# Linear attention on one core: shared copies and spare TensorE products in the last octet, and the fourth octet stored in five pieces

## The chip, the core and the metric

The kernel runs on one core of a Trainium2 chip. The metric is the device time in microseconds (us) of one execution. The kernel before takes 126.67 us, the median of 3 runs (126.56 to 126.73). A profile shows the span from the first to the last instruction of one execution, which is some 1.8 us shorter than that execution's time.

## The reference

```python
batch, heads, seq, dim = 8, 12, 512, 64                 # Q, K, V: float32
Q_feat = np.maximum(0, Q)
K_feat = np.maximum(0, K)
KV    = np.einsum('bhkd,bhkv->bhdv', K_feat, V)
K_sum = np.sum(K_feat, axis=2)
numerator   = np.einsum('bhqd,bhdv->bhqv', Q_feat, KV)
denominator = np.einsum('bhqd,bhd->bhq', Q_feat, K_sum)
return numerator / (denominator[:, :, :, None] + 1e-10)
```

There are 96 heads. The kernel handles them in twelve groups of eight, called octets, numbered 0 to 11 in the code; "the fourth octet" is `o == 3`, and the last is `o == NO - 1 == 11`.

## The kernel before

Each octet goes through the same steps: K and V are masked and multiplied (`mm_kv`), the sums are copied out of PSUM (`evac_kv`), Q is transposed and goes through the ReLU (`qt`), numerators (`out_t`) and denominators (`denom`) are computed, the numerators are transposed back (`back`), divided (`norm`) and stored (`store`). The order on each engine is the order of the program. All stores are issued by SyncE. Cuts are marked with `...`.

```python
    def evac_kv(o, gs):                       # four copies, all on ScalarE
        for s in range(2):
            for c in range(2):
                nc.scalar.copy(kvd[o % NK][64 * c:64 * c + 64, ...], ps_kv[64 * s:64 * s + 64, gs, ...])

    def qt(o):                                # Q transposed, ReLU on the way out of PSUM
        for i in range(2):
            ...                               # eight transposes into ps_qt
            if o == NO - 1 and i == 1:
                nc.vector.tensor_scalar(..., op0=Alu.max)
            else:
                nc.scalar.activation(qt_sb[o % NZ][:, us], ps, Act.Relu)

    def out_t(o):                             # numerators, two halves of four products each
        for j in range(2):
            ps = pou.tile([P, 4, U, 16], fp32, name="ps_ot", tag="ps_out")
            ...
            copy = nc.vector.tensor_copy if o == NO - 1 and j == 1 else nc.scalar.copy
            copy(ot[o][:, :, 4 * j:4 * j + 4], ps.rearrange("p h u c -> p u h c"))

    def store(o, o_sb):
        if o + DELAY < NO:
            nc.sync.dma_start(out=scratch, in_=k_sb[2 * (o + DELAY)][0:1, 0, :])
        Ov = Or[o].rearrange("p (r d) -> p r d", d=D)
        if o == NO - 1:                       # the last octet: two halves
            for j in range(2):
                rs = slice(RQ // 2 * j, RQ // 2 * (j + 1))
                nc.sync.dma_start(out=Ov[:, rs], in_=o_sb[:, rs])
            return
        nc.sync.dma_start(out=Ov, in_=o_sb)   # 1 MB: 128 partitions of 8 KB

    ...                                       # the end of the program, o = 10
    evac_kv(o + 1, slice(0, 1))
    prep(g + 1)
    prep_v(g + 1, nc.vector)
    backs(o)                                  # both halves: transposes back, norm, store
    mm_kv(g + 1)
    evac_kv(o + 1, slice(1, 2))
    qt(o + 1)
    out_t(o + 1)
    denom(o + 1)
    backs(o + 1)
```

The small store into `scratch` makes SyncE's queue wait for a later load; it only paces the stores.

## Time and profile before

| | before |
|---|---|
| time, median of 3 | 126.67 us |
| span of the profile | 124.92 us |
| TensorE, VectorE, ScalarE busy | 69%, 65%, 63% of the span |
| DMA engines busy | 90% or more in 37 of 40 slices |
| last landing of a store | 124.00 us |

The lines below are from the page of the profile before: the granted clock of TensorE and the busy share of the sixteen DMA engines, each over 40 slices of the span (a digit is a tenth), and a row of the store's issues (count, KB each, median us from issue to landing).

```profile
PEclk9999999999999999999859999657999999999687
DMA  3999999999999999999999999999999999999984
out_dram<-o_sb SPq DMA_DIRECT2D x11, 1024.0 KB, 9.1
```

No compute engine is near full, the DMA engines are full nearly throughout, and a store lands long after its issue: it stands in a queue. The clock falls in three places: near 62 us, near 79 us, and in the tail from 116 us on. The tail of the chain, the clock in it and the last three stores are shown inside the prediction below.

### The profile page before, as it was taken

Reading aid. Unit: us, or ns where it says so; the run is one execution under the profiler, and the core shown is the slowest. Engines: PE = TensorE matmul, PEld = TensorE weight load, DVE = VectorE, ACT = ScalarE, POOL = GpSimd, SP = SyncE. Lnnn points to the kernel's source line nnn. Section 1 sums busy time; section 2 is a strip of 40 time slices with the busy share of each in tenths; the row PEclk is TensorE's granted clock in tenths of the full one; section 3 lists DMA queues with packets and bytes.
Section 4 is the critical chain, followed back from the end, with each engine's and each line's share of the span. In section 5 each row is a group of like instructions: output and inputs, shape, how many; then the busy total and the mean of one; then the engine's idle time right before and its main releaser. Section 6 shows DMA issues by size and latency. Waiting matters only on the chain.

```text
span 124.9 us, 2637 instructions
## 1 busy us (share of the span) xinstructions
PE 86.0 (69%) x1056; PEld 78.7 (63%) x1056; DVE 81.6 (65%) x175; ACT 78.9 (63%) x115; POOL 31.3 (25%) x62
## 2 busy tenths in 40 slices
PE   0032297998989899894598596199867757795640
PEld 0041285997878789793597494199756566694630
DVE  2256644749798897979348759532946936994670
ACT  0163369969898998989339589164929928647000
POOL 6902424315253331142133124034022000000000
PEclk9999999999999999999859999657999999999687
DMA  3999999999999999999999999999999999999984
GB/s 102 380 310 214 215 207 210 217 205 214 207 212 211 208 217 326 255 216 297 286 213 284 304 211 252 332 212 234 339 226 217 323 259 216 314 425 420 428 352 197
DMA packets 10748, 32.68 MB, mean 262 GB/s; under 512 B 1392, under 2 KB 1392, under 8 KB 9328
## 3 DMA queue, kind: packets, MB, share of 16 engines
q0 software_dynamic: 8064, 17.83, 74.6%
q1 hardware_dynamic: 2384, 13.63, 27.2%
q10 hardware_dynamic: 288, 1.05, 2.1%
q8 instruction: 8, 0.13, 0.4%
q14 instruction: 4, 0.03, 0.1%
HBM read 37.75 MB, written 12.58 MB: 403 GB/s over the span
## 4 chain that ended last, share of the span: by engine, by line
DMA 34%; PE 28%; DVE 26%; ACT 6%; issue 2%; SPq 0%; DVEq 0%; ACTq 0%; POOLq 0%
DMA v_sb<-in_V_dram 14%; DMA q_sb<-in_Q_dram 13%; DVE o_sb L221 12%; PE ps_kv L148 11%; PE ps_bk L215 8%; DMA kv_first<-in_K_dram 7%; PE ps_qt L171 5%; DVE kf L134 4%; ACT qt L176 4%; PE ps_ot L187 3%; ACT kvd L157 2%; DVE vo L136 2%; DVE vo L143 2%; DVE den L205 1%; DVE rec L209 1%
## 5 line engine op out<-in xcount | busy, mean ns | idle before, releaser
L148 PE MATMUL ps_kv<-vo,kf 128*128 128x132 bf16 x384 | 31.0, 246 | 17.9 <-ACT vo L141 8.2
L148 PEld LDWEIGHTS <-kf 128*128 128x128 bf16 x384 | 28.5, 110 | 19.2 <-DVE vo L136 10.9
L221 DVE TENSOR_TENSOR o_sb<-ps_bk,rec 128x1024 f32<-128x1024 f32 x24 | 28.4, 1220 | 16.7 <-PE ps_bk L215 16.7
L157 ACT CAST kvd<-ps_kv 64x260 bf16<-64x260 f32 (+1 forms) x56 | 19.2, 342 | 18.8 <-PE ps_kv L148 16.1
L176 ACT ACTIVATE qt<-ps_qt 128x1024 bf16<-128x1024 bf16 x23 | 22.4, 1026 | 6.7 <-PE ps_qt L171 6.6
L215 PE MATMUL ps_bk<-ident,ot_sb 128*128 128x128 f32 x192 | 24.5, 284 | 1.1 <-DVE ot_sb L190 1.1
L190 ACT COPY ot_sb<-ps_ot 128x1024 f32<-128x1024 f32 x23 | 23.0, 1013 | 2.9 <-PE ps_ot L187 2.0
L134 DVE TENSOR_SCALAR kf<-k_sb,mask 128x1024 bf16<-128x1024 bf16 x44 | 18.3, 457 | 7.5 <-DMA k_sb<-in_K_dram 7.5
L215 PEld LDWEIGHTS ps_bk<-ident,ot_sb 128*128 128x128 f32 x192 | 22.4, 149 | 1.1 <-ACT ot_sb L190 1.1
L92 POOL DMA_DIRECT2D k_sb<-in_K_dram x22 | 11.9, 542 | 37.9 <-DMA q_sb<-in_Q_dram 20.6
L171 PE MATMUL ps_qt<-ident,q_sb 128*128 128x128 bf16 x192 | 15.2, 243 | 7.2 <-DMA q_sb<-in_Q_dram 7.2
L171 PEld LDWEIGHTS <-q_sb 128*128 128x128 bf16 x192 | 13.7, 110 | 8.2 <-DMA q_sb<-in_Q_dram 8.0
L187 PE MATMUL ps_ot<-qt,kvd 128*128 128x256 bf16 x96 | 14.5, 283 | 5.6 <-DVE o_sb L221 4.3
L94 POOL DMA_DIRECT2D v_sb<-in_V_dram x22 | 12.4, 562 | 17.5 <-DMA k_sb<-in_K_dram 9.5
L187 PEld LDWEIGHTS <-kvd 128*128 128x128 bf16 x96 | 9.3, 100 | 8.2 <-issue 6.1
L136 DVE TENSOR_SCALAR vo<-v_sb,mask 128x1024 bf16<-128x1024 bf16 x22 | 10.7, 488 | 1.5 <-DMA v_sb<-in_V_dram 1.5
L141 ACT ACTIVATE vo<-v_sb,mask 128x1024 bf16<-128x1024 bf16 x10 | 11.5, 1154 | 0.2
L197 PEld LDWEIGHTS <-qt 128*128 128x128 bf16 x192 | 6.8, 97 | 4.4 <-ACT qt L176 3.4
L197 PE MATMUL ps_den<-kvd,qt 128*128 128x16 bf16 x192 | 7.5, 180 | 2.4 <-ACT qt L176 2.1
L98 POOL DMA_DIRECT2D q_sb<-in_Q_dram x12 | 6.5, 544 | 8.2 <-DMA v_sb<-in_V_dram 5.3
L200 DVE SCALAR_TENSOR_TENSOR own<-ps_den,mask_h 128x256 f32<-128x256 f32 x12 | 5.0, 416 | 3.3 <-PE ps_den L197 3.3
L134 DVE TENSOR_SCALAR kf<-kv_first,mask 128x1024 bf16<-128x1024 f32 x4 | 2.8, 751 | 5.1 <-DMA kv_first<-in_K_dram 5.1
(22 smaller groups left out, 26.4 us busy)
## 6 DMA issues: line engine op xcount, KB each, us to landing
out_dram<-o_sb SPq DMA_DIRECT2D x11, 1024.0 KB, 9.1
q_sb<-in_Q_dram POOLq DMA_DIRECT2D x12, 512.0 KB, 14.7
k_sb<-in_K_dram POOLq DMA_DIRECT2D x22, 256.0 KB, 14.1
v_sb<-in_V_dram POOLq DMA_DIRECT2D x22, 256.0 KB, 13.2
kv_first<-in_V_dram ACTq DMA_DIRECT2D x2, 512.0 KB, 7.3
kv_first<-in_K_dram SPq DMA_DIRECT2D x2, 512.0 KB, 6.9
out_dram<-o_sb SPq DMA_DIRECT2D x2, 512.0 KB, 2.7
scratch<-k_sb SPq DMA_DIRECT2D x7, 0.1 KB, 4.8
```

The source lines that it names most:

```text
L94: nc.gpsimd.dma_start(out=v_sb[g].rearrange("p r d -> p (r d)"), in_=Vr[g])
L134: nc.vector.tensor_scalar(kf[g][:, :, s, :], k_sb[g], scalar1=0.0, scalar2=mask[:, 0, s:s + 1], op0=Alu.max, op1=Alu.mult)
L136: nc.vector.tensor_scalar(vo[g % NB][:, :, 0, 2:D + 2], v_sb[g], scalar1=mask[:, 1, 0:1], scalar2=None, op0=Alu.mult)
L148: nc.tensor.matmul(ps_kv[:, g % 2, 0:2 * (D + 2)].rearrange("p (t d) -> p t d", t=2), kf[g][:, r, :, :].rearrange("p s d -> p (s d)"), vo[ ...
L157: nc.scalar.copy(kvd[o % NK][64 * c:64 * c + 64, 4 * gs.start + s:4 * gs.stop:2, c * D1:c * D1 + D1].rearrange("p (g t) d -> p g t d", t=2 ...
L171: nc.tensor.transpose(ps[:, u, :], q_sb[o][:, i * (U // 2) + u, :], ident)
L176: nc.scalar.activation(qt_sb[o % NZ][:, us], ps, Act.Relu)
L187: nc.tensor.matmul(ps[:, i], kvd[o % NK][:, h, 1:2 * D + 1], q[:, :, h, :], start=True, stop=True, skip_group_check=True)
L190: copy(ot[o][:, :, 4 * j:4 * j + 4], ps.rearrange("p h u c -> p u h c"))
L197: nc.tensor.matmul(ps[:, u], qt_sb[o % NZ][:, u, :], kvd[o % NK][:, :, 0:2 * D1:2 * D1 - 1], start=True, stop=True, skip_group_check=True)
L215: nc.tensor.transpose(ps[:, 2 * v:2 * v + 2].rearrange("p c d -> p (c d)"), ot[o][:, 8 * j + v].rearrange("p h c -> p (h c)"), ident32)
L221: nc.vector.tensor_tensor(o_sb[:, rs], ps, rec[o][:, rs].unsqueeze(2).to_broadcast([P, 16, D]), op=Alu.mult)
```

## The change

The intent is in three parts. VectorE takes two of the last four evacuations, ScalarE takes over the last copy of the numerators (`ot`), and one normalisation moves, so that the last octet's products start sooner. TensorE runs eleven products whose results nobody reads ("spare products", `idle`) in its waits, so that its clock is not lowered. And the fourth octet's store is cut into 112 partitions and four pieces of 4, so that the DMA engines share its bytes unevenly.

```diff
+    ps_den = pde.tile([P, 2, 256], fp32, name="ps_den")
...
-    def evac_kv(o, gs):
+    def evac_kv(o, gs, share=False):
...
-                nc.scalar.copy(
+                copy = nc.vector.tensor_copy if share and c == 1 else nc.scalar.copy
+                copy(
...
+    def idle(n, o):
+        for i in range(n):
+            nc.tensor.matmul(ps_den[:, 1], ident, q_sb[o][:, 2 * i:2 * i + 2, :], start=True, stop=True,
+                             skip_group_check=True)
...
-            copy = nc.vector.tensor_copy if o == NO - 1 and j == 1 else nc.scalar.copy
-            copy(ot[o][:, :, 4 * j:4 * j + 4], ps.rearrange("p h u c -> p u h c"))
+            nc.scalar.copy(ot[o][:, :, 4 * j:4 * j + 4], ps.rearrange("p h u c -> p u h c"))
...
+    def cuts(o):
+        return ((16, P), (0, 4), (4, 8), (8, 12), (12, 16)) if o == 3 else ((0, P),)
...
-        nc.sync.dma_start(out=Ov, in_=o_sb)
+        for p0, p1 in cuts(o):
+            nc.sync.dma_start(out=Ov[p0:p1], in_=o_sb[p0:p1])
...
-    backs(o)
+    o_sb = out_tile()
+    norm(o, 0, back(o, 0), o_sb)
+    ps = back(o, 1)
     mm_kv(g + 1)
-    evac_kv(o + 1, slice(1, 2))
-    qt(o + 1)
-    out_t(o + 1)
+    evac_kv(o + 1, slice(1, 2), share=True)
+    for i in range(2):
+        relu_q(o + 1, i, transp(o + 1, i), nc.vector if i == 1 else None)
+    norm(o, 1, ps, o_sb)
+    store(o, o_sb)
+    idle(5, o + 1)
+    out_t(o + 1, (0,))
     denom(o + 1)
+    out_t(o + 1, (1,))
+    idle(6, o + 1)
     backs(o + 1)
```

More of the change, by code (lines that the diff above doesn't have):

```diff
@@ L162, in evac_kv, with transp, relu_q, out_t @@
                         "p g (t d) -> p g t d", t=2)[:, :, :, c:c + D1])
+    def transp(o, i):
+        ps = pqt.tile([P, U // 2, P], bf16, name="ps_qt")
+        for u in range(U // 2):
+            nc.tensor.transpose(ps[:, u, :], q_sb[o][:, i * (U // 2) + u, :], ident)
+        return ps
+    def relu_q(o, i, ps, eng=None):
+        to = qt_sb[o % NZ][:, i * (U // 2):(i + 1) * (U // 2)]
+        if eng is nc.vector:
+            nc.vector.tensor_scalar(to, ps, scalar1=0.0, scalar2=None, op0=Alu.max)
+        else:
+            nc.scalar.activation(to, ps, Act.Relu)
     def qt(o):
         for i in range(2):
-            us = slice(i * (U // 2), (i + 1) * (U // 2))
-            ps = pqt.tile([P, U // 2, P], bf16, name="ps_qt")
-            for u in range(U // 2):
-                nc.tensor.transpose(ps[:, u, :], q_sb[o][:, i * (U // 2) + u, :], ident)
-            if o == NO - 1 and i == 1:
-                nc.vector.tensor_scalar(qt_sb[o % NZ][:, us], ps, scalar1=0.0, scalar2=None,
-                                        op0=Alu.max)
-            else:
-                nc.scalar.activation(qt_sb[o % NZ][:, us], ps, Act.Relu)
-    def out_t(o):
-        ot[o] = otp.tile([P, U, 8, 16], fp32, name="ot_sb")
+            relu_q(o, i, transp(o, i))
+    def idle(n, o):
+        for i in range(n):
+            nc.tensor.matmul(ps_den[:, 1], ident, q_sb[o][:, 2 * i:2 * i + 2, :], start=True, stop=True,
+                             skip_group_check=True)
+    def out_t(o, halves=range(2)):
+        if halves[0] == 0:
+            ot[o] = otp.tile([P, U, 8, 16], fp32, name="ot_sb")
         q = qt_sb[o % NZ].rearrange("p u (h c) -> p u h c", h=8)
-        for j in range(2):
+        for j in halves:
             ps = pou.tile([P, 4, U, 16], fp32, name="ps_ot", tag="ps_out")
@@ L188, in out_t @@
                                  start=True, stop=True, skip_group_check=True)
-            copy = nc.vector.tensor_copy if o == NO - 1 and j == 1 else nc.scalar.copy
-            copy(ot[o][:, :, 4 * j:4 * j + 4], ps.rearrange("p h u c -> p u h c"))
+            nc.scalar.copy(ot[o][:, :, 4 * j:4 * j + 4], ps.rearrange("p h u c -> p u h c"))
     def denom(o):
-        ps = pde.tile([P, U, 8, 2], fp32, name="ps_den")
+        ps = ps_den[:, 0].rearrange("p (u h c) -> p u h c", u=U, h=8)
         for u in range(U):
```

## The prediction

> **What bounds the kernel now.** I read the chain of work that ended last first, because its end says which engine closes the program. In order of time (start us, length us, what), its last stretch, the tail of the twelfth octet, is:
>
> ```profile
> 112.78 0.27 ACT kvd L157
> 113.05 0.02 issue
> 113.07 1.03 ACT qt L176
> 114.10 0.04 issue
> 114.14 1.05 PE ps_ot L187 x8
> ...
> 115.28 1.23 DVE ot_sb L190
> 116.51 0.14 issue
> 116.65 3.47 PE ps_bk L215 x16
> 120.12 0.02 issue
> 120.14 1.23 DVE o_sb L221
> ```
>
> No transfer stands in it. Octet 12 goes from the evacuations (L157) through the ReLU (L176), the products (L187), a copy (L190) and sixteen transposes back (L215) to the last normalisation, which ends at 121.37. Next I asked the table of stretches for the clock (columns: stretch, its length, busy time and count of PE, weight loads, DVE, ACT, POOL, then granted clock, DMA share, GB/s).
>
> ```profile
> 107.80:110.40 2.60, 2.29 (x29) 2.29 (x29) 2.53 (x8) 2.05 (x6) 0.00 (x0) 1.00 1.03 395
> 112.80:116.60 3.80, 1.46 (x25) 1.35 (x24) 2.13 (x4) 2.28 (x3) 0.00 (x0) 0.97 1.00 420
> 116.60:120.10 3.50, 3.45 (x16) 3.25 (x16) 2.23 (x4) 0.00 (x0) 0.00 (x0) 0.55 0.97 407
> 121.40:124.10 2.70, 0.00 (x0) 0.00 (x0) 0.00 (x0) 0.00 (x0) 0.00 (x0) 0.83 0.70 284
> ```
>
> TensorE works 1.46 of 3.80 us, and then the granted clock is 0.55 just while the last transposes run: they take 3.46 us against 1.91 for the same sixteen at 109.05. That is the loss which the spare products aim at. But the DMA column says that the sixteen DMA engines are full (0.97 to 1.03) all the while, with stores queued since 103.66. So I asked for the issues of the last three stores (window at 113.0, at 119.9 and at 121.4; the last figure is us from issue to landing).
>
> ```profile
> out_dram<-o_sb SPq DMA_DIRECT2D x1, 1024.0 KB, 8.4
> out_dram<-o_sb SPq DMA_DIRECT2D x1, 512.0 KB, 2.8
> out_dram<-o_sb SPq DMA_DIRECT2D x1, 512.0 KB, 2.6
> ```
>
> The eleventh octet's store lands at 113.02 + 8.4 = 121.4, the halves of the twelfth at 119.88 + 2.75 = 122.63 and 121.40 + 2.6 = 124.00. In the records of the sixteen completion marks of each transfer, the stores before them land at 111.59, 114.04, 116.50, 118.96 and 121.39: one per 2.45 us, so one half per 1.23 us. With nothing to wait for but this queue, the halves would land at 121.39 + 1.23 = 122.62 and 123.85. The first does so exactly, the second is 0.15 us late. This is the reading that decides: the arithmetic tail and the drain of the stores end together, and a faster tail alone can win about 0.15 us, whatever it saves on TensorE.
>
> The marks also show that the engines are uneven. Those of the eleventh octet's store run from 119.82 to 121.39: the first engine is 1.57 us ahead of the last. Already from 52 us the marks of each K load spread over some 1.45 us, and each octet has a period of 10.0 us. Only the lagging engines set the end.
>
> **What the Trainium skill says.** "TensorE: Matmul & The Clock Gate", Part 1, says that the clock is halved after an insufficiently busy window of about 3.4 us and restored after a busy one. The trace agrees: the clock records change at 116.37 and 119.78, 3.41 us apart, to 0.5 and back. The window before (112.96 to 116.37) held some 1.4 us of TensorE work, 41%. "DMA: Bandwidth & Descriptors", "Why a DMA increments its semaphore by 16 and not by 1", says that a transfer uses the largest number of engines up to 16 that divides its slowest dimension, and on a hardware queue the lowest-numbered ones: 112 partitions give sixteen engines seven rows each, and each piece of 4 gives four rows to engines 0 to 3 only. No trace yet shows a transfer of that form. The same page, "Latency and other measured facts", calls engines 7 and 15 usually slower; the spread above agrees that some lag, but the marks carry no engine's number. "PSUM — Partial Sum Buffer", "PSUM bank collisions raise a hardware error", wants accesses to one bank ordered; no run here has tried one, but it bears on the spare products, which write the bank that VectorE's denominator reads.
>
> **Part 1, the shared copies.** In before, ScalarE does four evacuations of 0.27 us, 111.95 to 113.05, then the ReLU until 114.10. In the order of instructions of the changed kernel, two copies move to VectorE, but each waits for the one before on the other engine: ScalarE, VectorE, ScalarE, VectorE in series. VectorE's time I estimate from two rows of its groups: 256 elements from PSUM take 0.416 us, 1024 take 1.222, so 1.05 ns each and 0.145 fixed; 130 elements: 0.28. With some 0.06 us per hand-over, ScalarE's ReLU starts after three copies, 111.95 + 3 x 0.275 + 2 x 0.06 = 112.90, ends at 113.93; VectorE's fourth copy ends near 113.23 and its ReLU (0.69) near 113.93. The products start near 113.98, not 114.14: 0.15 us gained, not the half microsecond which sharing suggests.
>
> **Part 2, the moved normalisation.** Octet 11's second normalisation (1.22 us) now follows VectorE's ReLU: 113.95 to 115.18. Its PSUM buffer is needed by the second half of the products, which waits for it: first half 113.98 to 114.58, denominators (0.58) to 115.16, second half 115.22 to 115.82. Both copies of ot are now ScalarE's: 114.65 to 115.66 and about 115.9 to 116.9. So the transposes start near 117.0, 0.35 us later than before. VectorE's denominator chain (0.42 + 0.42 + 0.35) is then done by 116.5 and out of the way.
>
> **Part 3, the spare products.** Five of 128x256 follow the transposes of Q, which end near 112.8. From eight such products in 1.03 us, five take 0.65 us and fill a wait until 113.98 that they don't lengthen. Six (0.75 us) follow the second half; they wait for the denominator's read (done near 115.65), start near 115.85 and end at 116.6, before the transposes can start. In the window to 116.37 TensorE is now busy for about 0.5 + 0.6 + 0.58 + 0.6 + 0.5 = 2.8 of 3.41 us, 82%, so I expect the full clock. Then eight transposes take 0.95 us: 117.0 to 117.95, a normalisation to 119.2, the second to 120.45. The last store is issued near 120.5, 0.9 us earlier than 121.40, and a store into an idle queue lands 2.6 us later: 123.1.
>
> **Part 4, the cut store.** The fourth octet's store is issued at 73.48. Engines 4 to 15 get seven rows of 8 KB instead of eight, 0 to 3 get eleven. A store of eight rows takes 2.45 us, so a row is 0.31 us: minus 0.31 on twelve engines, plus 0.92 on four. Four more issues of 0.53 us on the store's queue delay nothing (the next store is at 83.4). Since the drain is limited by the last engine, and the queues never run dry from here on, the 0.31 us would be kept to the end if the four are among those that lead by at least 1.2 us. In the marks of the eleventh store, six engines lead the last one by 0.9 us or more (119.82 to 120.50), five of them by over 1.0. The change was presumably chosen by trial, so I take it at 80% that the four are leaders. The loads land earlier too, but after 80.75 the chain holds no transfer, so that is worth nothing.
>
> **The sum.** Drain without the cut: 123.85, which is 0.15 under 124.00. With the cut, 123.85 - 0.31 = 123.54, so 0.46 less. The tail's own 123.1 is below either. 126.67 - 0.46 = 126.2; weighted with the chance that the cut gives less, 126.3 us.
>
> **Rivals.** (a) The tail counts in full: if stores were only waiting for arithmetic, 0.9 us would be saved: 125.8. For it speaks the chain, which ends in arithmetic; against it the landings, 2.45 us apart without a gap. (b) Engines 0 to 3 are not leaders: then a lagging engine carries 0.92 us more and the end moves to 124.8, 127.4 us. For it speaks that I can't name the engines; against it that somebody kept the change. (c) The clock falls anyway, since windows run free of the program: transposes from 117.0 at half clock end at 120.5, the last normalisation at 121.8, the landing at 124.4: 127.0 us. Against it: 82% is near twice the 41% that lost the clock. (d) The stall at 80.75, where TensorE waited 3.1 us for Q and ran at clock 0.50 from 78.82 to 85.65, might shift. It costs about 2 us of arithmetic; but the cut doesn't speed that very load. Each lagging engine has some 1.45 us of it left when the store comes (about 77.5), five packets of 0.31 us taken in turn with five of the store's: fewer than the seven that remain.
>
> **Range and chances.** The drain fixes the centre at 126.2 to 126.5, (a) bounds it below, (b) and (c) above. I take 125.8 to 126.9 for 8 in 10. Over 2% would be 2.5 us either way; no part sums to it. Faster 0.03, same 0.95, slower 0.02.
>
> **What would show it.** Right: the clock stays at 1.0 from 113 to 120; the sixteen transposes take about 1.9 us; the last normalisation ends near 120.5; VectorE's copies alternate with ScalarE's; the last two stores land one drain step apart, near 123.5; and the marks after 82 us spread less. Wrong: the last landing follows the last issue by 2.6 us (arithmetic still the bound), the spread grows to over 2 us (rival b), or the clock shows 0.5 after 116 (rival c).

## The result, and the profile after

The changed kernel takes 127.59 us (median of 6 runs, 127.48 to 127.73). The kernel before, run beside it, takes 126.7. The ratio is 1.0067, with a 95% interval of 1.0046 to 1.0087: within 2%, but clearly slower, by about 0.85 us. A ratio here and below is the mean time of one kernel's fast runs over that of the kernel before's fast runs of the same rounds, so it is not quite the ratio of the medians quoted beside it.

The last lines of the chain of work that ended last, in the changed kernel (start us, length us, what):

```profile
110.89 0.28 ACT kvd L160
111.16 0.02 issue
111.19 0.30 DVE kvd L160
111.48 0.02 issue
111.51 0.28 ACT kvd L160
111.78 0.02 issue
111.81 0.30 DVE kvd L160
112.11 0.03 issue
112.14 0.69 DVE qt L177
112.83 1.14 DVE o_sb L234
113.97 0.04 issue
114.02 0.63 PE ps_ot L201 x4
114.64 0.02 issue
114.66 1.02 ACT ot_sb L203
115.69 0.04 issue
115.73 1.11 PE ps_bk L228 x8
116.84 0.02 issue
116.86 1.22 DVE o_sb L234
118.08 1.13 DVEq L358
```

The copies alternate between ScalarE and VectorE, the moved normalisation stands between the ReLU and the second half of the products, and TensorE's last transposes start at 115.73. The last line is VectorE's sequencer, which waits for the second of the last two normalisations. In the timeline of those microseconds the sixteen transposes take 1.97 us together instead of 3.46, and the last normalisation ends at 119.22 instead of 121.37. The arithmetic of the last octet is done 2.1 us earlier, in a kernel that is slower.

The table of stretches of the changed kernel (columns as in the prediction; whose nearest stretch starts at 112.80):

```profile
113.00:116.60 3.60, 3.05 (x38) 2.54 (x37) 2.15 (x4) 2.02 (x2) 0.00 (x0) 1.00 1.02 430
116.60:120.10 3.50, 1.09 (x11) 0.86 (x8) 2.36 (x2) 0.00 (x0) 0.00 (x0) 1.00 1.01 421
120.10:124.00 3.90, 0.00 (x0) 0.00 (x0) 0.00 (x0) 0.00 (x0) 0.00 (x0) 0.65 0.73 299
```

TensorE is busy 3.05 of 3.60 us where it was below half before, and the clock is 1.00 right through the last transposes (0.55 before). The DMA share is still 1.0 until 120.1, and from there on nothing but DMA works.

The issues of the last three stores of the changed kernel, in windows at 114.0, 118.1 and 119.2:

```profile
out_dram<-o_sb SPq DMA_DIRECT2D x1, 1024.0 KB, 8.2
out_dram<-o_sb SPq DMA_DIRECT2D x1, 512.0 KB, 5.3
out_dram<-o_sb SPq DMA_DIRECT2D x1, 512.0 KB, 5.4
```

The halves of the last octet waited 5.3 and 5.4 us for their landing, where they took 2.8 and 2.6 before. The earlier arithmetic was turned into a longer queue. The last half lands at 119.24 + 5.41 = 124.65, against 124.00.

Why it lands later is in the completion marks of the sixteen DMA engines, one mark per engine and transfer (times in us, sorted; the trace gives no engine's number). For the eleventh octet's store and the last half:

```
before    11th  119.82 ... 121.28 121.32 121.33 121.39      last half  123.83 ... 123.97 123.97 124.00
after     11th  119.59 ... 121.25 121.33 121.44 122.21      last half  122.07 ... 123.74 123.78 123.92 124.65
```

After the change, fifteen engines are done at 123.92, and one stands alone 0.73 us behind. The marks of the eleventh store now spread over 2.62 us instead of 1.57. From the last landing to the end of the span it takes 1.15 us instead of 0.91. Both have to be explained.

### The profile page after: what moved, and what is told of

Its sections match the earlier page's. It is cut to its first block, busy times and chain, and to the rows that moved or that the text cites. A ratio compares the mean times of both kernels' runs of the same rounds, so it can differ in the third digit from the quotient of the medians.

```text
span 125.8 us, 2663 instructions
## 1 busy us (share of the span) xinstructions
PE 84.5 (67%) x1067; PEld 76.8 (61%) x1067; DVE 81.1 (64%) x176; ACT 79.2 (63%) x114; POOL 30.9 (25%) x62
## 4 chain that ended last, share of the span: by engine, by line
DMA 33%; DVE 31%; PE 21%; ACT 5%; issue 2%; DVEq 1%; SPq 0%; ACTq 0%; POOLq 0%
DMA v_sb<-in_V_dram 13%; DVE o_sb L234 13%; DMA q_sb<-in_Q_dram 12%; PE ps_kv L150 11%; DMA kv_first<-in_K_dram 7%; PE ps_bk L228 7%; DVE kf L136 5%; ACT kvd L160 3%; DVE vo L138 3%; PE ps_qt L171 3%; DVE vo L145 2%; DVE den L218 2%; DVE rec L222 2%; DVE own L213 2%; ACT qt L179 2%
## 5 line engine op out<-in xcount | busy, mean ns | idle before, releaser
L150 PE MATMUL ps_kv<-vo,kf 128*128 128x132 bf16 x384 | 30.0, 241 | 17.8 <-ACT vo L143 8.3
L150 PEld LDWEIGHTS <-kf 128*128 128x128 bf16 x384 | 27.4, 107 | 19.1 <-DVE vo L138 10.9
L160 ACT CAST kvd<-ps_kv 64x260 bf16<-64x260 f32 (+1 forms) x54 | 18.7, 346 | 17.6 <-PE ps_kv L150 14.8
L203 ACT COPY ot_sb<-ps_ot 128x1024 f32<-128x1024 f32 x24 | 24.0, 1014 | 3.0 <-PE ps_ot L201 2.0
L228 PE MATMUL ps_bk<-ident,ot_sb 128*128 128x128 f32 x192 | 23.3, 275 | 0.4 <-ACT ot_sb L203 0.4
L228 PEld LDWEIGHTS ps_bk<-ident,ot_sb 128*128 128x128 f32 x192 | 21.2, 143 | 0.7 <-ACT ot_sb L203 0.7
L201 PE MATMUL ps_ot<-qt,kvd 128*128 128x256 bf16 x96 | 13.9, 271 | 4.9 <-DVE o_sb L234 4.3
```

The source lines that it names most:

```text
L150: nc.tensor.matmul(ps_kv[:, g % 2, 0:2 * (D + 2)].rearrange("p (t d) -> p t d", t=2), kf[g][:, r, :, :].rearrange("p s d -> p (s d)"), vo[ ...
L160: copy(kvd[o % NK][64 * c:64 * c + 64, 4 * gs.start + s:4 * gs.stop:2, c * D1:c * D1 + D1].rearrange("p (g t) d -> p g t d", t=2), ps_kv[6 ...
L201: nc.tensor.matmul(ps[:, i], kvd[o % NK][:, h, 1:2 * D + 1], q[:, :, h, :], start=True, stop=True, skip_group_check=True)
L203: nc.scalar.copy(ot[o][:, :, 4 * j:4 * j + 4], ps.rearrange("p h u c -> p u h c"))
L228: nc.tensor.transpose(ps[:, 2 * v:2 * v + 2].rearrange("p c d -> p (c d)"), ot[o][:, 8 * j + v].rearrange("p h c -> p (h c)"), ident32)
```

## The experiments

Twelve kernels were run, ten of them several times, the two probes (e5, e6) once each; "gap" is the time from the last landing to the end of the span.

### 1. Which part of the change did it: e1_nocut and e2_cut_only

e1_nocut is the changed kernel with the fourth octet whole again. e2_cut_only is the kernel before with the cut alone.

```diff
 e1_nocut (against the changed kernel)
-        return ((16, P), (0, 4), (4, 8), (8, 12), (12, 16)) if o == 3 else ((0, P),)
+        return ((16, P), (0, 4), (4, 8), (8, 12), (12, 16)) if o == -1 else ((0, P),)
 e2_cut_only (against the kernel before)
-        nc.sync.dma_start(out=Ov, in_=o_sb)
+        for p0, p1 in (((16, P), (0, 4), (4, 8), (8, 12), (12, 16)) if o == 3 else ((0, P),)):
+            nc.sync.dma_start(out=Ov[p0:p1], in_=o_sb[p0:p1])
```

> The changed kernel with the fourth store whole again (copies shared, spare products kept). Theory A, the cut costs: engines 0 to 3 carry three rows more (0.92 us) to the end, and one of them is the engine that ends alone at 124.65; without the cut the last landing goes back to 123.85, so 126.4 to 126.6 us. Theory B, the earlier tail costs: [...]last fetch of program (8 KB at 118.93, before at 120.19) now falls among queued stores whatever the cut does; then 127.3 to 127.6 us, as the changed kernel.

> The kernel before with nothing but the cut of the fourth store. Theory A: the engine that ends last carries the rows too, 127.3 to 127.7 us. Theory B: the fetch comes at about 120.2 as before, 126.5 to 126.8 us. The prediction's own view (the four are leaders) would be 126.4.

Measured: e1_nocut 126.59 us (126.55 to 126.69), ratio 0.9992 (0.998 to 1.0004). e2_cut_only 127.70 us (127.64 to 127.82), ratio 1.0079 (1.0066 to 1.0092).

The whole loss is the cut: 127.59 - 126.59 = 1.00 us with the new tail, and about as much with the old one. The tail alone wins nothing that is clear of the noise. The chain of e1_nocut ends like that of the changed kernel:

```profile
115.60 1.11 PE ps_bk L228 x8
116.71 0.02 issue
116.73 1.23 DVE o_sb L234
117.96 1.13 DVEq L358
```

Its last normalisation ends at 119.09, 2.3 us before that of the kernel before, and its last store is issued at 119.11 instead of 121.40. Its marks show where this went: the eleventh store lands at 121.38, the halves at 122.69 and 123.87. The prediction's drain without arithmetic was 122.62 and 123.85. So the drain sets the end, and the tail's 2.3 us became 0.13 us.

e2_cut_only lands at 124.81, 0.81 us after the kernel before. One engine stands alone in its first half (123.44, the next at 122.69), but the sixteen marks of its last half lie together, 124.59 to 124.81. Its packets end at 124.22 on one engine and by 123.87 on the others; why the other marks came as late as that one's was not found. So the last marks show one engine behind with the new tail, and not with the old one.

### 2. The tail's own parts: e3_noidle and e4_copies_only

e3_noidle is the changed kernel without the eleven spare products. e4_copies_only also has the fourth octet whole.

```diff
-    idle(5, o + 1)
+    idle(0, o + 1)
...
-    idle(6, o + 1)
+    idle(0, o + 1)
```

> The changed kernel without its eleven spare products. If they hold the clock, the last sixteen transposes go from 1.97 us to about 3.5 us and the last normalisation ends 1.5 us later, near 120.7; the time is set by the drain, so theory A says 127.4 to 127.7 us, unchanged; theory B says less, 126.7 to 127.1 us, as the fetch is late again.

> The changed kernel with the fourth store whole and without spare products: only the shared copies and the moved normalisation. Both theories: within 0.2 us of before, 126.5 to 126.9 us, with the clock halved in the last transposes.

Measured: e3_noidle 127.64 us (127.58 to 127.69), ratio 1.0073 (1.006 to 1.0086). e4_copies_only 127.01 us (six runs from 126.64 to 128.19), ratio 1.0041 (1.0009 to 1.0074).

The chain and a stretch of e3_noidle:

```profile
116.13 0.04 issue
116.18 3.69 PE ps_bk L228 x16
119.87 0.02 issue
119.89 1.22 DVE o_sb L234
```

```profile
116.60:120.10 3.50, 3.25 (x16) 2.85 (x14) 1.44 (x2) 0.00 (x0) 0.00 (x0) 0.50 0.95 398
```

Without the spare products the clock is 0.50 and the sixteen transposes take 3.69 us instead of 1.97. The spare products do what they were written for, and the time is the same (127.64 against 127.59), since the last landing is (124.68 against 124.65). With the fourth octet whole, their worth can't be read off: e4_copies_only scatters over 1.5 us around a median just above the expected range, and its profiled run has a late program fetch (explained in part 4) at 124.04 which moved its last landing to 125.49. That run is inconclusive about the spare products.

### 3. How the cut's rows fall on the engines: e7, e8 and e9

e7_cut_twice cuts the sixth octet too, so that engines 0 to 3 get the extra rows twice. e8_cut_eights cuts 16 partitions into two pieces of 8, which gives engines 0 to 7 one row more and the others one less. e9_pairs puts 0.94 us of extra rows on engines 0 and 1 alone and takes 0.13 us from the other fourteen.

```diff
 e7_cut_twice
-        return ((16, P), (0, 4), (4, 8), (8, 12), (12, 16)) if o == 3 else ((0, P),)
+        return ((16, P), (0, 4), (4, 8), (8, 12), (12, 16)) if o in (3, 5) else ((0, P),)
 e8_cut_eights
+        return ((16, P), (0, 8), (8, 16)) if o == 3 else ((0, P),)
 e9_pairs (with the cut above off)
+        if o == 3:
+            cut = RQ - 14
+            nc.sync.dma_start(out=Ov[:, 0:cut], in_=o_sb[:, 0:cut])
+            for p0, p1 in [(16, P)] + [(p, p + 2) for p in range(0, 16, 2)]:
+                nc.sync.dma_start(out=Ov[p0:p1, cut:RQ], in_=o_sb[p0:p1, cut:RQ])
+            return
```

> The changed kernel with the sixth store cut in the same way too. Theory A (rows stay on engines 0 to 3 to the end): another 0.92 us, 128.3 to 128.7 us. Rival D (only the chance meeting with a fetch costs): 127.4 to 127.8 us as the changed kernel, whose other engines get another 0.31 us less.

> The changed kernel with the fourth store as 112 partitions and two pieces of 8: engines 0 to 7 have nine rows, 8 to 15 seven. Theory A: engines 0 to 3 have only 0.31 us more instead of 0.92, so the lone engine ends about 0.6 us earlier, 126.6 to 127.1 us. Rival (the small transfers themselves cost): 127.4 or more.

> The changed kernel with another cut of the fourth store: of the last 896 elements of each row, partitions 16 to 127 go over sixteen engines and the first sixteen in eight pieces of 2, so engines 0 and 1 carry 3.06 rows more (0.94 us), as the four of the cut do, and 2 to 15 carry 0.44 rows less (0.13 us). The probe saw that the engine which ends alone is 2 or 3, and that 0 and 1 stand about 0.7 and 1.1 us ahead of the last. Theory A: the lone engine isn't loaded now, and the end moves by -0.1 to +0.3 us against the whole store: 126.5 to 126.9 us, no mark standing alone by 0.7 us. Rival (any engine that carries three rows more costs as much): 127.4 to 127.8 us.

| kernel | time, us | ratio (95%) | marks of the last half, the latest ones |
|---|---|---|---|
| e7_cut_twice | 128.41 (128.23 to 128.5) | 1.012 (1.0104 to 1.0135) | twelve to 123.19, then 124.50 124.79 125.05 125.78 |
| e8_cut_eights | 127.16 (127.0 to 127.38) | 1.0026 (1.0013 to 1.0038) | all to 123.96, none alone |
| e9_pairs | 127.27 (127.14 to 127.44) | 1.0046 (1.0032 to 1.0059) | 124.14, 124.21, none alone |

e7_cut_twice shows the four engines with the extra rows directly: exactly four marks stand apart by 1.3 us. It also confirms that the pieces of four partitions all run on the same four engines, since nothing else would single out four. A slower end with more of the same cut says that these four are no leaders with room to spare.

e8_cut_eights and e9_pairs took 0.06 and 0.37 us more than the top of their expected ranges. Their last landings are only 0.09 and 0.34 us behind that of e1_nocut; most of the rest is the gap, 1.27 and 1.33 us against 0.90 (part 6). The time of e9_pairs lies between what its theory and its rival expected and decides nothing by itself; that no mark stands alone speaks for the theory.

### 4. Where engines 0 to 3 stand: e5_probe_nocut and e6_probe_after

To name engines, the eleventh octet's store ends in a last row that is cut as 112 partitions, then 8, 4, 2 and 2 partitions. By the rule for the choice of engines that the prediction quotes, these small pieces run on engines 0 to 7, 0 to 3, and 0 and 1. The trace gives no engine's number; the counts of marks (8, 4, 2 and 2) agree. Their marks show when just those engines come to that place in the queue. e5 has the fourth octet whole and the same probe there too, e6 has it cut.

```diff
 e5_probe_nocut (with the cut off); e6_probe_after: `o in (10,)`, with the cut
+        if o in (3, 10):
+            last = RQ - 1
+            nc.sync.dma_start(out=Ov[:, 0:last], in_=o_sb[:, 0:last])
+            for p0, p1 in ((16, P), (0, 8), (8, 12), (12, 14), (14, 16)):
+                nc.sync.dma_start(out=Ov[p0:p1, last:RQ], in_=o_sb[p0:p1, last:RQ])
+            return
```

> A measurement. The changed kernel with the fourth store whole; the fourth and the eleventh store give up their last 256 bytes of each row to five tiny transfers, of 112, 8, 4, 2 and 2 partitions, whose completion marks come from engines 0 to 15, 0 to 7, 0 to 3, 0 and 1, 0 and 1. So the marks tell for the first time where the low engines stand. Theory A (four middling engines are loaded): at the eleventh store the four marks of engines 0 to 3 lie some 0.9 to 1.2 us ahead of the last of the sixteen. Rival C (they already lag): they are among the last. Prediction's view (they lead): they are the first four.

> The same probe on the eleventh store of the changed kernel itself, with its cut. Theory A: the four marks of engines 0 to 3 are now at the end, and the engine that ends alone (0.77 us after the other fifteen) is one of them. Rival D (the lone engine is any engine that the program fetch hits): the lone mark is not among the four.

Each was run once (127.08 and 127.86 us; the probe's own pieces cost some time), so these are readings of marks, not of times:

```
e5, uncut:  large part of the store, 16 engines   119.83 ... 121.47
            piece of 4 (engines 0 to 3)           120.92 121.11 121.35 122.04
            piece of 2 (engines 0 and 1)          121.10 121.54
e6, cut:    large part of the store, 16 engines   ... 121.32 122.22
            piece of 4 (engines 0 to 3)           121.64 121.75 121.85 122.79
            piece of 2 (engines 0 and 1)          121.83 122.03
```

A small piece adds about 0.19 us, and the piece of 4 is the third one. Taking 3 x 0.19 off, engines 0 to 3 are at 120.35, 120.54, 120.78 and 121.47 at the end of the large part in e5, when the last engine of all is at 121.47. So three of them lead the last by 1.12, 0.93 and 0.69 us, and the fourth by nothing. The cut puts 0.92 us on each. They do not lead by the 1.2 us that the prediction needed. The expectation, 0.9 to 1.2 us for all four, held for two of them.

In e6 the engine that stands alone (122.22 and 122.79) is among the four marks of the piece of 4 but not among the two of engines 0 and 1. It is engine 2 or 3, if the rule holds.

The records of single packets tell why one of these engines has no lead. One of the few packets that aren't data is a fetch of the program itself. The page of the changed kernel lists these by queue (number, MB, share of the sixteen engines):

```profile
q8 instruction: 8, 0.13, 0.4%
q14 instruction: 4, 0.03, 0.1%
```

Those of the second queue have 8 KB each. The last of them, in the packet records of the changed kernel:

```
start us   queue         took ns   bytes
118.93     instruction   309       8192
119.23     store         664       8192     (median of the store's packets: 309)
```

The fetch and the slowed packet right behind it cost one engine 309 + (664 - 309) = 664 ns. That is near the distance at which one mark stands alone in the store then running (122.21 - 121.44 = 0.77), and in the store before it none stands alone (118.97 and 118.98 are the last). That the packets belong to the engine of this mark is inferred from the times. e5 shows the same: a fetch at 119.69, a slow packet of 646 ns after it, and one of engines 0 to 3 at the very end. In e5 the fourth engine's missing lead thus already contains the fetch. In e1_nocut the fetch came at 122.21 and no engine ended alone, which fits an engine that leads as the other three do and has no extra rows; its number I could not read there. e4 and e10 have no extra rows either, but their fetch (124.04 and 121.97) fell into a last half whose engines started level: the marks of the half before lie together, 122.75 to 122.93 and 121.33 to 121.51. In both, one engine ended alone, 0.97 and 0.94 us behind. So a fetch can do it without extra rows, where the engines have no lead left.

The tenth store, which landed before this fetch, shows what the rows cost without it: 118.98 in the changed kernel, 118.93 in e1_nocut, 118.96 in the kernel before. With one cut the rows cost next to nothing by themselves (with two, in e7_cut_twice, that store lands at 120.12). They used up the lead of these engines, and the fetch then came on top. In the kernel before, the fetch at 120.19 stays hidden: no mark stands alone. This account of the fetch is read from marks; no run moved the fetch alone.

This reading can be checked on e7_cut_twice, whose four engines carry 2 x 0.92 = 1.84 us. Estimated from e1_nocut's last landing (123.87) and the four leads of e5 (1.12, 0.93, 0.69, 0): 124.59, 124.78, 125.02 and 125.71. The marks are 124.50, 124.79, 125.05 and 125.78. For the changed kernel the same sum gives 123.87 + 0.92 - 0 = 124.79 for the one alone; it is 124.65. e9_pairs, whose engines 0 and 1 carry 0.94 us but not the fetch, ends without a lone engine at 124.21.

What sets the moment of that fetch stayed open. In the fourteen profiles the last such fetch starts between 112.94 and 124.04.

### 5. Does the time follow the queue's bytes: e10_nocut_less and e11_before_less

These two store only half of the eleventh octet, so their result is wrong. That takes one half, 1.23 us of drain, out of the queue.

```diff
+        if o == NO - 2:
+            nc.sync.dma_start(out=Ov[:, 0:RQ // 2], in_=o_sb[:, 0:RQ // 2])
+            return
```

> Wrong result on purpose: the kernel with shared copies and spare products, fourth store whole, but the eleventh store writes only the first half of each row: 512 KB less in the queue, 1.23 us of drain. If the drain sets its end and the arithmetic tail has 2 us in hand, the whole 1.23 us is won: 125.2 to 125.5 us. If the tail set the end, nothing is won: 126.6.

> Wrong result on purpose: the kernel before with the same 512 KB left out. Its last store is issued at 121.40 and lands 2.6 us later, only 0.15 us after what the queue would allow; so the arithmetic tail should hold it and at most 0.15 us be won: 126.5 to 126.8 us. If the drain alone set its end: 125.4.

Measured: e10_nocut_less, with the new tail, 126.21 us (126.41, 126.01, 125.94 and 127.05), ratio 0.9971 (0.9936 to 1.0005). e11_before_less, with the old tail, 126.80 us (126.85, 126.84, 126.76 and 125.69), ratio 0.9986 (0.9954 to 1.0018).

e10 stays 0.7 us above its expected range. With the old tail, 1.23 us less to drain changes three of four runs by nothing (the fourth, 125.69, had a mean clock of 0.945 against 0.927): there the last store is issued at 121.57 in the profiled run and lands 2.6 us later, so the arithmetic is right behind the drain. With the new tail some of it shows. In the profiled run fifteen engines end at 122.78, 1.1 us earlier than in e1_nocut, and one alone at 123.72, after the program fetch at 121.97. Both intervals reach 1, so this pair agrees with a tie of drain and arithmetic in the kernel before, and proves it less well than the landings do.

### 6. The last quarter microsecond: e12_four_more

The lone engine explains 124.65 - 123.87 = 0.78 us of the 1.00. The rest is after the last landing. SyncE ends the program with one wait for each of the eight completion semaphores that its transfers use in turn, in a fixed order, some 0.06 us each (two first loads that ScalarE issues take two of the turns). Four more transfers move the last store from the eighth semaphore to the fourth, so the waits for four other semaphores, long since complete, stand behind the last landing instead of before it. To test it without moving a single row, e12_four_more leaves the fourth octet whole and adds four transfers of 128 bytes behind its store.

```diff
 e12_four_more (with the cut off)
+    extra = [consts.tile([1, D], bf16, name=f"extra{i}") for i in range(4)]
...
+        if o == 3:
+            for x in extra:
+                nc.sync.dma_start(out=x, in_=k_sb[2 * (o + DELAY)][0:1, 0, :])
```

> The changed kernel with the fourth octet whole (as e1_nocut) and, after that store, four more transfers of 128 bytes each into rows that nothing else needs, so that the number of transfers is that of the cut but no row changes its engine. Theory (part of the loss is the order of SyncE's closing waits): four more transfers move the last store from the eighth completion semaphore to the fourth, so four or five of SyncE's closing waits of 0.06 us come after the last landing instead of before: last landing as in e1_nocut (about 123.87), 0.2 to 0.3 us more after it, 126.8 to 126.9 us against 126.6 of e1_nocut. Rival (the number of transfers costs nothing; the whole loss was in the landings): 126.5 to 126.7 us, and 0.87 us from the last landing to the end of the span as in e1_nocut.

Measured: 127.06 us (126.93 to 127.10, 6 runs), ratio 1.0026 (1.0013 to 1.0039). SyncE's instructions after the last landing, from the trace:

```
e1_nocut       landing 123.87   waits 123.89                                    drain 123.96   end 124.77
e12_four_more  landing 124.17   waits 124.19 124.25 124.31 124.37 124.43        drain 124.50   end 125.33
after          landing 124.65   waits 124.67 124.72 124.79 124.84 124.91        drain 124.97   end 125.80
```

The five waits and the longer gap (1.16 us against 0.90) are there, as in the changed kernel, without any row moved. The same holds in every profile:

| transfers on SyncE's queue | semaphore of the last store | waits after the last landing | gap, us | profiles |
|---|---|---|---|---|
| 22 or 30 | eighth | 1 | 0.90 to 0.91 | before, e1, e4, e7, e10, e11 |
| 26 | fourth | 5 | 1.15 to 1.16 | after, e2, e3, e12 |
| 24 or 32 | second | 7 | 1.27 to 1.28 | e8, e5 |
| 31 | first | 8 | 1.33 to 1.34 | e9, e6 |

e7_cut_twice has eight transfers more, and its gap is that of the kernel before: what counts is the place in the order and not the number.

The expectation for e12 missed in one thing. Its time is above the expected range and 0.47 us above that of e1_nocut, and its last landing, which should have stayed, is 0.30 us later. Of these, 0.25 us are already there when the last load of K lands (105.56 against 105.31), and 0.09 at the first load of Q (11.08 against 10.99), before any store. Why the loads of this kernel run later I could not settle, so its time by itself does not prove the 0.25 us; the gap does.

## Why the prediction was wrong

The record says 126.3 us, 125.8 to 126.9. The result is 127.59 us, outside the range, though within 2% as the chances had it. Point by point, by the prediction's own steps:

- **What bounds the kernel: right.** "The arithmetic tail and the drain of the stores end together, and a faster tail alone can win about 0.15 us." In e1_nocut the drain took over at 123.87, against 123.85 worked out beforehand, and the last landing came 0.13 us earlier. Rival (a), the tail counting in full, is refuted by the same run.
- **Parts 1 and 2, copies and normalisation: right in shape, within 0.2 us in length.** Counted from the first of the four copies, I had the ReLU done after 1.98 us, the second half of the products begun after 3.27, the transposes after 5.05 and the last normalisation done after 8.50. The trace has 1.94, 3.13, 4.84 and 8.33. In absolute time all of it is a further 1.06 us earlier, because the stall at 80 us, the prediction's point (d), shifted the good way: the clock came back at 83.75 instead of 85.65. That was luck and not the change: it came back at 83.57 in e1_nocut, without the cut, at 86.18 in e2_cut_only, with it, and at 85.84 in e12, which has the new tail. None of this reached the end of the program.
- **Part 3, spare products: right.** TensorE was busy 3.05 of 3.60 us and kept the full clock until 121.3; without them (e3_noidle) it ran at 0.50. As the Trainium skill says ("TensorE: Matmul & The Clock Gate", Part 1), the clock followed how busy the window was. The page's table speaks of an idle window; in the kernel before, a window with 42% of TensorE work (1.45 of 3.41 us) was followed by the half clock. Rival (c) did not occur. Denominator and spare products share a PSUM bank; VectorE's read ended at 114.37 and the first of the six spare products began at 114.46, so they were ordered as the Trainium skill's page "PSUM — Partial Sum Buffer" ("PSUM bank collisions raise a hardware error") wants, and every run was correct but e10 and e11.
- **Part 4, the cut store: the step that failed.** It reads "The change was presumably chosen by trial, so I take it at 80% that the four are leaders." That the pieces all run on the same four engines was right (their numbers no trace shows). That these lead by 1.2 us was a guess about who made the change, put in the place of a measurement, and it was wrong. In e5 three of the four lead by 0.69 to 1.12 us, and one, after its fetch, by nothing; each got 0.92 us. The term that was booked as -0.31 us measured +0.78 us at the last landing. This is rival (b), which I put at 127.4 us and gave too little weight, and its sign came true: the marks of the eleventh store spread over 2.62 us. That it came out so near is partly luck: (b) had no fetch in it.
- **"Four more issues ... delay nothing": wrong by 0.25 us.** They delayed no store, but they shifted the last one from the eighth closing wait to the fourth. I had not looked at what SyncE does after the last landing. No rival contained it.

The sum of what the runs show, from e1_nocut to the changed kernel: 0.78 us at the last landing and 1.15 - 0.90 = 0.25 us behind it make 1.03, against 1.00 measured. From the kernel before, the tail gives back 0.13 us of this at the last landing, which is not clear of the noise in the times. The expected gain of the tail was not lost to a slow engine: it went into a longer wait in the queue, 5.4 us instead of 2.6 for the last half.

What stays open: what sets the time of the program fetch and why it falls on engine 2 or 3, why all marks of e2's last half were late, and why the loads of e12 were late. The best version is the changed kernel with the fourth octet whole (126.59 us), which is not clear of the kernel before.

## What to carry to other kernels

When the arithmetic and the drain of the stores end together, speeding up the arithmetic alone only lengthens the queue; look at the time from issue to landing before and after to see it. Before moving bytes from one DMA engine to another, measure which engine lags, with a small piece that only some engines carry, and count in the program fetches that share the engine. And look behind the last landing: a change in the number of transfers can move the last one in the order of the closing waits, which cost 0.06 us per wait here.

## What the Trainium skill lacked or had wrong

- "DMA: Bandwidth & Descriptors", "Why a DMA increments its semaphore by 16 and not by 1", gives the lowest-numbered engines for a hardware queue as seen for 16, 10, 2 and 1 engines. Here pieces of 4 partitions left four marks and pieces of 8 left eight, and in e7_cut_twice exactly four marks stood 1.3 us apart. No trace here gives an engine's number.
- The same page, "Latency and other measured facts", names engines 7 and 15 as usually slower. No run here shows whether these two lag. The engine that ended alone, 0.73 us behind, was engine 2 or 3 by the numbering above, made late by extra rows and, as far as the marks show, a program fetch. No page that I read warns of that combination.
- "Runtime: NRT & Kernel Launch", "Instruction fetch mechanics", says that a sequencer fetches its program in 16 KB blocks by its own DMA queue while it executes. The trace has eight such transfers of 16 KB, and four of 8 KB, a size that the page doesn't have. It does not say what a fetch costs other transfers: here 0.31 us for 8 KB, plus 0.36 us on the store packet behind it (664 ns instead of 309).
- No page that I read tells how the order of the closing waits adds to a kernel's end: 0.06 us for each semaphore waited for after the one of the last store, 0.90 us from the last landing to the end with one such wait and 1.34 us with eight.
